# Thirty gathered rows of the first layer given out later: the count EARLY goes from 302 to 272

## The chip, the cores and the metric

The kernel runs on one core of a Trainium2 chip. The metric is the device time of one execution in microseconds (us); lower is better. The core's engines each run their own queue of instructions: TensorE (PE; its weight loads are listed apart as PEld), VectorE (DVE), ScalarE (ACT), GpSimd (POOL) and SyncE (SP), which here issues DMAs. They wait for each other and for DMAs by semaphores.

## The reference

A backbone of two layers over 512 latent tokens and 256 context tokens, width 1024, in float32. Context tokens read only context; latent tokens read both.

```
for i in range(2):
    xl = rmsnorm(hl, norm1_g[i]) * (1 + scale) + shift      # latent; the same for the context (xc)
    yl, yc = even_mixer(...) if i == 0 else odd_mixer(...)  # mLSTM + differential attention; windowed attention with sinks
    hl = hl + gate * yl                                     # output projection inside the mixer
    xl = rmsnorm(hl, norm2_g[i]) * (1 + scale) + shift
    hl = hl + gate * peer(xl)
    if i == 0:
        hc = hc + gate * yc
        hc = hc + gate * peer(rmsnorm(hc) ...)
out = rmsnorm(hl, final_g)
```

The part that matters is `peer`, a layer of 16384 experts of one neuron each. For each token, 8 heads pick 16 experts each by product keys (128 x 128 keys), so 128 pairs of rows (u, v) per token:

```
a = einsum('nd,nhkd->nhk', x, u[eidx])        # 128 dot products of 1024 for each token
w = gate * gelu(a)
y = einsum('nhk,nhkd->nd', w, v[eidx])        # 128 rows, weighted and added
```

## The kernel before

Tokens are handled in blocks of 128: two of context, four of latent tokens. The program runs in this order: the context through the first mixer, its output projection and its choice of experts; the latent tokens through the first mixer (`even`); their output projection (`out_proj`, line 836); `peer` of the first layer (line 1340); the second layer's windowed attention (`odd`, line 1183) and its output projection; `peer` of the second layer.

**Two ways to compute the experts.** For three of the four latent blocks of the first layer (384 tokens) all experts are computed, *densely*: the loop over 128 key blocks j takes 128 experts at a time. TensorE multiplies the 384 tokens by the block's u rows (`dA`, line 217), ScalarE applies Gelu (`dz`), VectorE multiplies with the gates (`dz`, line 1168), which are zero for experts that weren't picked, and splits the result into a high and a low part (`dw`, lines 1171 and 1172); TensorE multiplies by the block's v rows and adds into `dacc` (line 1178). The rows themselves are loaded (`draw`) and split too (`dhi` on ScalarE, `dlo` on VectorE or GpSimd, lines 1122 and 1123). The last four j (TAIL) are accumulated block by block. Behind the loop, for each of the three blocks, `resid` (line 1046) computes `hm`, the sum times a gate row `m` (line 1052), and adds it to the residual `hr` (line 1053).

For the two context blocks and the last latent block the picked rows are *gathered*. The generator `gather` (line 1003) hands out one row per token at each `next(rows)`: an indirect DMA that GpSimd issues (line 1010; 128 x 1024 float32, 524,288 bytes) into a ring of five buffers `uv`, and one pass on VectorE. For each block come 128 u rows (a dot product with the token, `junkv` and `pa`, line 1023), then 128 v rows (weighted and added into `pacc`, line 1036). Three blocks make 768 such steps, in one fixed order: block by block, u before v. In these texts each such step is called a row. The buffers for `hm`, `hr` and `m` of `resid` come from the same ring of five.

**Where the rows are given out.** The 768 are spread over five places by counts. EARLY rows are handed out in `run` (line 1447) ahead of the latent mixer, with a late priority: they fill VectorE and DMA time wherever the mixer and the output projection leave room. GROWS, 48, come beside the building of the gates (`beside`, line 1362). LATE, 64, come inside `odd`. What is left is spread over the dense loop:

```
left, done = 256 * len(gat) - done - GROWS[l] - late, 0
...
while done < min(left * (j + 2) // GEND, left):
    next(rows)
```

with GEND = 124, each batch held until the low part of `dw` of block j has been issued.

**What sets the order.** The program's text gives the instructions in one order with priorities; a scheduler with its own simulated timeline then decides, before the kernel is run, in which order each engine's instructions stand. An engine executes its queue strictly in that order. So a row given out at one place of the text can stand elsewhere in the queues.

**Around the two ends.** In `out_proj` each of the four latent blocks gets its product `ops` (line 223, four column quarters), VectorE multiplies it with a gate row (`ot`, line 852) and adds it to the residual (`oh`, line 853). Then each block is normed (`norm`, lines 372 to 381: the squares on ScalarE, L377; `xn` on VectorE, lines 379 and 381), transposed on TensorE (`xps`, line 388) and split into a high part on ScalarE (`xth`, line 393) and a low part on VectorE (`xtl`, line 394). `xn` has two buffers. Then the first score projection of `peer` begins (`pqps`, line 217).

Behind the dense part, the two context blocks are loaded again and normed (`xn`; here line 381's addition runs on GpSimd) and transposed into `xt` (copied by ScalarE, line 390); their keys are TensorE's `okps` (line 210). The latent blocks' norms start from `hr`. A few small constants for the attention are made on VectorE: `bfc` (line 1213) and the sinks `snp`, `snk`, `snr` (lines 1205 to 1210). `rt` (line 725) belongs to the rotation of the first queries and keys of the heads.

Of the kernel before, what the change touches and what calls it, by code (L numbers as in the profile page):

```python
# [24 lines left out]
SEGS = [(0, 1, 16), (1, 2, 8), (2, 4, 5), (4, 8, 3), (8, 16, 1)]  # L25
NCAND = sum((b - a) * n for a, b, n in SEGS)
UPRE = 18, 27
EARLY = 302
GROWS = 48, 0
LATE = 64  # L30
F5 = [], [5]
# [79 lines left out]
class Kern:  # L111
# [1299 lines left out]
    def run(self, out):  # L1411
# [12 lines left out]
        with self.mixing():  # L1424
            with self.tc.tile_pool(name="even", bufs=1, reuse_waits="tile") as self.pe:
# [20 lines left out]
                with self.later():  # L1446
                    for _ in range(EARLY):
                        next(rows)
# [4 lines left out]

        self.peer(0, xt, 2, gat, rows, EARLY, LATE, put)
        with self.phase("n1c"):
# [93 lines left out]
```

## Time and profile before

| | us |
|---|---|
| median of three runs | 4182.2 (4175.84 to 4185.61) |
| the profiled execution, by the same clock as the runs | 4186.29 |
| span of its trace (first to last instruction) | 4184.5 |
| TensorE busy | 3808.1 (91%) |
| VectorE busy | 3281.6 (78%) |
| GpSimd busy | 2266.9 (54%) |
| ScalarE busy | 1526.5 (36%) |
| 512 gathers of u rows, GpSimd's time for them | 670.2 |
| 512 gathers of v rows, GpSimd's time for them | 684.1 |

The profile is of one execution, the table's second line; the sums below are made against it. Busy times of engines overlap, so they do not add up to the span. The 1024 gathers are those of both layers.

### The profile page before, as it was taken

To read this page: it belongs to the slowest core of one execution; us is meant where nothing else is said; L and a number is where in the kernel's file an instruction comes from. 1 tells how busy PE (TensorE), PEld (TensorE's weight loads), DVE (VectorE), ACT (ScalarE), POOL (GpSimd) and SP (SyncE) were. 2 spreads that over 40 slices of the span, in tenths; PEclk is the share of its full clock that TensorE was granted. 3 is DMA by queue.
4 is the path that set the end of the run, shared out by engine and by line. 5 is a ranking of instruction groups with operands and counts; after the bars stand their busy time and mean duration, and the time that the engine had idled before them with its cause. 6 is when DMAs were issued, how large, how long until landed. Compare 5 with 4: busy or idle time off the path is not lost.

```text
span 4184.5 us, 56313 instructions
## 1 busy us (share of the span) xinstructions
PE 3808.1 (91%) x19774; PEld 3252.5 (78%) x19780; DVE 3281.6 (78%) x5763; ACT 1526.5 (36%) x2798; POOL 2266.9 (54%) x1644
## 2 busy tenths in 40 slices
PE   8988777758899899999999889999999999999999
PEld 5776554546687799999889777777887899999987
DVE  4259888977988899999989987537955977777788
ACT  3322322412156433333333324332366333333333
POOL 1016767554453588778778563004531766666664
PEclk9999988878999999999999999999999999999999
DMA  5556888786339999989899995423346978788778
GB/s 193 171 201 207 314 316 308 263 314 234 129 121 371 361 326 346 350 310 343 317 332 331 341 332 194 154 90 112 117 161 241 347 275 285 275 288 278 280 266 314
DMA packets 389674, 1099.30 MB, mean 263 GB/s; under 512 B 32959, under 2 KB 140807, under 8 KB 383246
## 3 DMA queue, kind: packets, MB, share of 16 engines
q0 software_dynamic: 147456, 536.94, 35.4%
q1 hardware_dynamic: 232142, 497.95, 34.8%
q10 hardware_dynamic: 9792, 60.82, 3.5%
q8 instruction: 155, 2.54, 0.2%
q14 instruction: 129, 1.06, 0.1%
HBM read 1024.18 MB, written 71.40 MB: 262 GB/s over the span
## 4 chain that ended last, share of the span: by engine, by line
PE 55%; DMA 14%; DVE 13%; issue 10%; POOL 7%; ACT 2%; SPq 0%; POOLq 0%; ACTq 0%; DVEq 0%
PE dacc L1178 19%; PE dA L217 17%; DMA uv<-in_pr_u_dram,ix 4%; POOL uv L1010 4%; DMA uv<-in_pr_v_dram,ix 3%; PE pqps L217 2%; DMA draw<-in_uT_dram 2%; PE ops L223 2%; PE gps L1108 2%; DVE junkv L1023 2%; PE oo L1335 1%; PE gds L1091 1%; PE ops L1305 1%; PE modps L252 1%; PE vps L223 1%
## 5 line engine op out<-in xcount | busy, mean ns | idle before, releaser
L1178 PE MATMUL dacc<-dhi,dw 128*128 128x512 f32 x3072 | 986.6, 391 | 5.6 <-ACT dw L1171 3.8
L1010 POOL DMA_INDIRECT uv<-in_pr_u_dram,ix x512 | 670.2, 1309 | 463.0 <-DVE pa L1023 330.4
L1010 POOL DMA_INDIRECT uv<-in_pr_v_dram,ix x512 | 684.1, 1336 | 399.6 <-DVE pacc L1036 274.3
L1023 DVE CUSTOM_DVE_ANT_0 junkv<-uv,x 128x1024 bf16<-128x1024 f32 x512 | 695.1, 1358 | 60.1 <-DMA uv<-in_pr_u_dram,ix 55.9
L1036 DVE SCALAR_TENSOR_TENSOR pacc<-uv,pw,pacc 128x1024 f32<-128x1024 f32 x508 | 701.3, 1381 | 42.0 <-DMA uv<-in_pr_v_dram,ix 38.1
L1178 PEld LDWEIGHTS dacc<-dhi,dw 128*128 128x128 f32 x3072 | 578.5, 188 | 122.5 <-ACT dw L1171 4.5
L1123 POOL TENSOR_TENSOR dlo<-draw,dhi 128x1024 fp32r<-128x1024 f32 x210 | 542.3, 2583 | 211.4 <-ACT dhi L1122 207.7
L1122 ACT CAST dhi<-draw 128x1024 fp32r<-128x1024 f32 x467 | 489.5, 1050 | 445.2 <-issue 176.1
L1178 PE MATMUL dacc<-dlo,dw 128*128 128x512 f32 x1536 | 603.9, 393 | 7.2 <-DVE dlo L1123 7.2
L1168 DVE TENSOR_TENSOR dz<-dz,dG 128x384 f32<-128x384 f32 x256 | 406.5, 1601 | 79.0 <-ACT dz L1138 75.1
L1171 ACT CAST dw<-dz 128x384 fp32r<-128x384 f32 x256 | 131.4, 514 | 708.2 <-PE dacc L1178 690.3
L217 PE MATMUL dA<-xth,dhi 128*128 128x384 f32 x1688 | 335.3, 340 | 11.6 <-ACT dhi L1122 9.8
L1123 DVE TENSOR_TENSOR dlo<-draw,dhi 128x1024 fp32r<-128x1024 f32 x257 | 322.2, 1254 | 27.5 <-ACT dhi L1122 26.7
L1178 PEld LDWEIGHTS dacc<-dlo,dw 128*128 128x128 f32 x1536 | 289.1, 188 | 66.2 <-DVE dlo L1123 9.7
L217 PEld LDWEIGHTS dA<-xth,dhi 128*128 128x128 f32 x1688 | 306.5, 189 | 28.7 <-ACT dhi L1122 10.2
L217 PE MATMUL dA<-xtl,dhi 128*128 128x384 f32 x1688 | 327.4, 335 | 0.0
L217 PE MATMUL dA<-xth,dlo 128*128 128x384 f32 x1688 | 326.6, 334 | 0.8 <-POOL dlo L1123 0.8
L217 PEld LDWEIGHTS dA<-xtl,dhi 128*128 128x128 f32 x1688 | 296.7, 188 | 0.1
L217 PEld LDWEIGHTS dA<-xth,dlo 128*128 128x128 f32 x1688 | 295.6, 188 | 1.2 <-POOL dlo L1123 1.1
L1172 DVE TENSOR_TENSOR dw<-dz,dw 128x384 fp32r<-128x384 f32 x256 | 162.8, 636 | 151.5 <-ACT dw L1171 151.5
L1108 PEld LDWEIGHTS gps<-ghot 128*128 128x128 f32 x1536 | 202.2, 192 | 49.9 <-issue 21.9
L196 POOL TENSOR_TENSOR wlo<-wraw,whi 128x1024 fp32r<-128x1024 f32 x55 | 132.9, 2418 | 194.7 <-ACT whi L195 121.3
(341 smaller groups left out, 6044.9 us busy)
## 6 DMA issues: line engine op xcount, KB each, us to landing
draw<-in_pr_v_dram SPq DMA_DIRECT2D x256, 512.0 KB
draw<-in_uT_dram SPq DMA_DIRECT2D x211, 512.0 KB
wraw<-in_wb_dram SPq DMA_DIRECT2D x150, 512.0 KB
gd<-gch ACTq DMA_DIRECT2D x48, 1024.0 KB
dG<-gd SPq DMA_DIRECT2D x30, 1536.0 KB
wraw<-in_mod_t_dram SPq DMA_DIRECT2D x48, 512.0 KB
wraw<-in_uT_dram SPq DMA_DIRECT2D x45, 512.0 KB
wraw<-in_mod_w_dram SPq DMA_DIRECT2D x32, 512.0 KB
```

The source lines that it names most:

```text
L196: eng.tensor_tensor(lo, raw, hi.bitcast(F32), op=OP.subtract)
L217: self.nc.tensor.matmul(ps, w[wi][:, k, :], x[xi][:, k, 0:T], start=(i == 0), stop=(i == 23))
L1010: nc.gpsimd.indirect_dma_start(out=t, out_offset=None, in_=a[table], in_offset=bass.IndirectOffsetOnAxis(ap=ix[:, c:c + 1], axis=0))
L1023: nc.vector.tensor_tensor_reduce(out=junk, in0=u, in1=x, op0=OP.mult, op1=OP.add, scale=1.0, scalar=0.0, accum_out=A[:, c:c + 1])
L1036: nc.vector.scalar_tensor_tensor(acc, v, W[:, c:c + 1], acc, op0=OP.mult, op1=OP.add)
L1108: nc.tensor.matmul(ps[0][:, t0 % 8 + t, :], h[0][:, t, :], h[1][:, t, :], start=True, stop=True)
L1122: nc.scalar.copy(hi, raw)
L1123: eng.tensor_tensor(lo, raw, hi.bitcast(F32), op=OP.subtract)
L1168: nc.vector.tensor_tensor(z3, z3, self.G[:, :, j % JG, :], op=OP.mult)
L1171: nc.scalar.copy(wh, z)
L1172: i = nc.vector.tensor_tensor(wl, z, wh.bitcast(F32), op=OP.subtract)
L1178: self.nc.tensor.matmul(acc[b][:, h, :], w[wi][:, 128 * b:128 * b + 128], v[vi][:, 512 * h:512 * h + 512], start=(j == 0 and i == 0), stop ...
```

## The change

One number: of the 768 rows of the first layer, 272 and not 302 are handed out ahead of the latent mixer. GROWS and LATE stay, so the rest, which the dense loop spreads, is 384 and not 354.

```diff
 UPRE = 18, 27
-EARLY = 302
+EARLY = 272
 GROWS = 48, 0
 LATE = 64
```

Where the rows come to stand is decided by the scheduler, so here is the order of the instructions of both kernels at three places. (`uv<-in_pr_u_dram` is a gather of u rows, `uv<-in_pr_v_dram` one of v rows; `x21` means that the instruction stands 21 times in a row; a row's dot product shows as two lines, `junkv,pa` and `pa`.)

GpSimd's queue from the last part of the latent mixer to the start of the choice of experts, as one piece of the difference:

```order
 L736 MEMSET qpd 64x512
 L1010 DMA uv<-in_pr_v_dram,ix 128x1024 x59
-L1010 DMA uv<-in_pr_u_dram,ix 128x1024 x51
+L1010 DMA uv<-in_pr_u_dram,ix 128x1024 x21
 L196 TENSOR_TENSOR wlo<-wraw,whi 128x1024 x4
 L955 MEMSET sel 128x4
```

The 59 gathers of v rows in front stay; of 51 gathers of u rows 21 stay.

VectorE's queue at the end of the output projection of the first layer, before (`oh_6039` to `oh_6041` are the residuals of three of the four blocks, `x_3582` the context block whose dot products the rows make):

```order
L852 TENSOR_TENSOR ot<-ops,mr 128x256
L379 SCALAR_TENSOR_TENSOR xn<-oh_6039,rstd,mr 128x1024
L1023 ISA junkv,pa<-uv,x_3582 128x1024
L1023 ISA pa 128x1
L853 TENSOR_TENSOR oh_6041<-oh_6041,ot 128x256
L379 SCALAR_TENSOR_TENSOR xn<-oh_6040,rstd,mr 128x1024
L381 TENSOR_TENSOR xn<-xn,mr 128x1024
L1023 ISA junkv,pa<-uv,x_3582 128x1024
L1023 ISA pa 128x1
L852 TENSOR_TENSOR ot<-ops,mr 128x256
```

The same place of the changed kernel (`oh_5919` to `oh_5922` are the residuals of the blocks):

```order
L852 TENSOR_TENSOR ot<-ops,mr 128x256
L853 TENSOR_TENSOR oh_5920<-oh_5920,ot 128x256
L379 SCALAR_TENSOR_TENSOR xn<-oh_5919,rstd,mr 128x1024
L381 TENSOR_TENSOR xn<-xn,mr 128x1024
L379 SCALAR_TENSOR_TENSOR xn<-oh_5920,rstd,mr 128x1024
L852 TENSOR_TENSOR ot<-ops,mr 128x256
L381 TENSOR_TENSOR xn<-xn,mr 128x1024
L853 TENSOR_TENSOR oh_5921<-oh_5921,ot 128x256
L852 TENSOR_TENSOR ot<-ops,mr 128x256
L853 TENSOR_TENSOR oh_5922<-oh_5922,ot 128x256
L394 TENSOR_TENSOR xtl<-xps,xth 128x8x128 x2
```

Between the projection's products and norms stood dot products of rows; now none do. The first 16 rows of this block stand earlier on VectorE in both kernels, in the same places.

VectorE's queue behind the dense loop, before (the first line here are the last rows behind the last `dw`; `dacc_10198` to `dacc_10200` are the three dense blocks' sums):

```order
L1123 TENSOR_TENSOR dlo<-draw,dhi 128x1024
L1036 SCALAR_TENSOR_TENSOR pacc<-uv,pw,pacc 128x1024 x10
L1213 TENSOR_SCALAR bfc<-cst 128x128 x4
L1052 TENSOR_TENSOR hm<-dacc_10198,m_18841 128x1024
L1036 SCALAR_TENSOR_TENSOR pacc<-uv,pw,pacc 128x1024
L1053 TENSOR_TENSOR hr<-hr,hm 128x1024
L1052 TENSOR_TENSOR hm<-dacc_10199,m_18841 128x1024
L1053 TENSOR_TENSOR hr<-hr,hm 128x1024
L1052 TENSOR_TENSOR hm<-dacc_10200,m_18841 128x1024
L1205 TENSOR_SCALAR snr<-snr 128x16
L379 SCALAR_TENSOR_TENSOR xn<-xn,rstd,mr 128x1024
```

The same place of the changed kernel:

```order
L1123 TENSOR_TENSOR dlo<-draw,dhi 128x1024
L1036 SCALAR_TENSOR_TENSOR pacc<-uv,pw,pacc 128x1024 x10
L1213 TENSOR_SCALAR bfc<-cst 128x128 x4
L1036 SCALAR_TENSOR_TENSOR pacc<-uv,pw,pacc 128x1024 x5
L379 SCALAR_TENSOR_TENSOR xn<-xn,rstd,mr 128x1024
...
L1208 SCALAR_TENSOR_TENSOR snk<-snp,cst,snk 128x16
L1036 SCALAR_TENSOR_TENSOR pacc<-uv,pw,pacc 128x1024 x22
L1052 TENSOR_TENSOR hm<-dacc_10078,m_18841 128x1024
L1052 TENSOR_TENSOR hm<-dacc_10079,m_18841 128x1024
L1053 TENSOR_TENSOR hr<-hr,hm 128x1024 x2
L1052 TENSOR_TENSOR hm<-dacc_10080,m_18841 128x1024
```

The first `hm` stood behind 15 rows and the four `bfc`; now it stands behind 19 rows, the context norm, the sink constants and 22 rows more. Counted over the whole queue, 338 rows stand between the first and the last `dw` before (the 351st to the 688th of the 768), and 343 in the changed kernel (the 321st to the 663rd); behind the last `dw` and ahead of the attention's own rows (LATE) stand 16 before and 41 now. The queues of TensorE, ScalarE and SyncE read almost the same in both, but for SyncE's loads behind the dense loop: `m` and `hr` stood ahead of the context's loads and now stand behind them (`mr`, `xn<-h`, `snr`, three weights, `mrow`). On ScalarE the squares of `hr` stand ahead of the copies of the context's transposes (L390) in both. On TensorE `okps` stands behind the third block's transposes in both.

## Rows read from the trace of the kernel before

**Rows 1.** The page: span, and busy time of each engine.
```profile
span 4184.5 us, 56313 instructions
PE 3808.1 (91%) x19774; PEld 3252.5 (78%) x19780; DVE 3281.6 (78%) x5763; ACT 1526.5 (36%) x2798; POOL 2266.9 (54%) x1644
```
**Rows 2.** Windows: length, PE PEld DVE ACT POOL busy, granted clock, DMA share, GB/s.
```profile
921.00:993.00 72.00, 49.78 (x218) 41.39 (x217) 62.17 (x104) 11.95 (x22) 39.60 (x34) 0.84 0.93 345
1350.00:1400.00 50.00, 39.82 (x248) 34.25 (x248) 32.47 (x52) 26.77 (x37) 15.99 (x14) 0.93 1.03 399
1450.00:2300.00 850.00, 841.78 (x4242) 764.38 (x4242) 784.05 (x754) 306.55 (x410) 674.15 (x396) 1.00 0.92 331
2390.00:2453.00 63.00, 38.69 (x156) 29.07 (x156) 46.23 (x44) 14.88 (x31) 34.20 (x23) 0.78 0.91 337
2453.00:2560.00 107.00, 98.06 (x618) 82.66 (x617) 98.00 (x116) 42.78 (x122) 62.98 (x74) 0.98 0.91 332
```
**Rows 3.** Dense part: chain, then (1450 to 2300 us) gather queue, VectorE's rows.
```profile
1450.34 4.12 PE dacc L1178 x18
1454.46 4.18 PE dA L217 x24
...
q0 software_dynamic: 42531, 154.87, 49.7%
...
L1036 DVE SCALAR_TENSOR_TENSOR pacc<-uv,pw,pacc 128x1024 f32<-128x1024 f32 x146 | 231.3, 1584 | 1.0
```
**Rows 4.** Lines from 926 to 993.5 us: busy, mean ns, idle and releasers.
```profile
L223 PE MATMUL ops<-wraw,xt 128*128 128x256 f32 x162 | 37.9, 394 | 6.3 <-DVE ot L852 4.5 <-DMA wraw<-in_wb_dram 1.8
L388 PE MATMUL xps<-cst,xn 128*128 128x128 f32 x32 | 6.9, 389 | 13.5 <-DVE xn L381 13.5
L217 PE MATMUL pqps<-xth,whi 128*128 128x512 f32 x2 | 1.2, 696 | 2.5 <-DVE xtl L394 2.5
...
L1023 DVE CUSTOM_DVE_ANT_0 junkv<-uv,x 128x1024 bf16<-128x1024 f32 x30 | 36.8, 1228 | 6.8 <-DMA uv<-in_pr_u_dram,ix 6.6
```
**Rows 5.** Behind the dense part: VectorE in time order, lines 2366.5:2393, gathers 2366:2388.
```profile
2366.32 0.56 DVE L1172 TENSOR_TENSOR dw<-dz,dw 128x384 fp32r<-128x384 f32 x1 [0.67 <-ACT dw L1171]
2393.07 0.62 DVE L1213 TENSOR_SCALAR bfc<-cst 128x128 bf16<-128x128 f32 x4
2394.50 1.23 DVE L1052 TENSOR_TENSOR hm<-dacc,m 128x1024 f32<-128x1024 f32 x1 [0.81 <-DMA m<-modd]
2403.18 1.28 DVE L379 SCALAR_TENSOR_TENSOR xn<-xn,rstd,mr 128x1024 f32<-128x1024 f32 x1
2408.88 2.39 DVE L1208 SCALAR_TENSOR_TENSOR snk<-snp,cst,snk 128x16 bf16<-128x16 bf16 x1
...
2452.88 0.55 DVE L725 TENSOR_TENSOR rt<-rps,cst 128x384 f32<-128x384 f32 x1
...
L1036 DVE SCALAR_TENSOR_TENSOR pacc<-uv,pw,pacc 128x1024 f32<-128x1024 f32 x15 | 19.3, 1288 | 3.9 <-DMA uv<-in_pr_v_dram,ix 3.7
L1123 DVE TENSOR_TENSOR dlo<-draw,dhi 128x1024 fp32r<-128x1024 f32 x3 | 3.7, 1219 | 0.0
...
L1010 POOL DMA_INDIRECT uv<-in_pr_v_dram,ix x12 | 16.7, 1392 | 6.1 <-DVE pacc L1036 4.0 <-issue 2.1
```
**Rows 6.** Behind the dense part: ScalarE, GpSimd, TensorE in order of time.
```profile
2400.97 1.06 ACT L377 ACTIVATE junk<-xn 128x1024 bf16<-128x1024 f32 x1 [25.76 <-DMA xn<-h]
2403.95 1.04 ACT L377 ACTIVATE junk<-hr 128x1024 bf16<-128x1024 f32 x1
2408.94 1.01 ACT L390 COPY xt<-xps 128x1024 f32<-128x1024 f32 x1 [1.93 <-PE xps L388]
...
2404.54 2.34 POOL L381 TENSOR_TENSOR xn<-xn,mr 128x1024 f32<-128x1024 f32 x1 [1.08 <-DVE snp L1207]
...
2406.94 1.97 PE L388 MATMUL xps<-cst,xn 128*128 128x128 f32 x8 [16.50 <-POOL xn L381]
2414.37 10.12 PE L210 MATMUL okps<-xt,wraw 128*128 128x256 f32 x32 [1.10 <-ACT xt L390]
```

## The prediction

> **What bounds the kernel now.** I read the page first, then the table of windows stage by stage, then the waits and the order of time at the two ends of the change. TensorE is busy in 91% of the span [rows 1], so what counts is where it is not.
>
> The dense part of the first layer is TensorE's: 841.78 of 850 us busy, at the full clock [rows 2], and its chain is nothing but 4.18 us of `dA` and 4.12 us of `dacc` by turns, 8.30 us for one of 128 key blocks [rows 3]. Beside it VectorE is busy 784.05 us (66 idle) and the DMA engines 0.92 of the time (68 us idle) at 331 GB/s: both have room, but little.
>
> The latent output projection is otherwise: from 926 to 993.5 us TensorE sits idle for 6.3 + 13.5 + 2.5 = 22.3 us, waiting for VectorE (`ot`, `xn`, `xtl`) and once for a weight, while VectorE works through 30 gathered rows, 36.8 us of them [rows 4], and the DMA share is 0.93 [rows 2].
>
> A third place matters, which the words of the change do not name: the seam between the dense part and the second layer. From 2390 to 2453 us TensorE is busy 38.69 of 63 us [rows 2]. What releases it starts with `hm`, the residual of the dense blocks (L1052), at 2394.50 [rows 5].
>
> **The change, part by part.** Nothing is computed less: 30 rows, each one gather on GpSimd, 0.52 MB of DMA and one VectorE pass, are given out later.
>
> *Out of the projection.* GpSimd's order shows 21 gathers for 51 there. VectorE's first 16 rows stand where they stood, so up to about 925 us nothing changes; the 30 after that are gone. Of TensorE's 22.3 us the 6.3 before `ops` should go, as `ot` and `oh` no longer stand behind rows. Of the 16.0 us around the four norms a part stays: the third norm hangs on ScalarE's order and on the write of the first `xn` out of its buffer (two buffers for four blocks), and its own steps get no shorter by an empty queue. I take 6 of the 16 as gained, so **12 us gained**; bounds: 4.5 (only the waits for `ot`) and all 22.3.
>
> *Into the dense part.* Here I counted VectorE's order instead of trusting the loop. Between the first and the last `dw` stand 688 - 350 = 338 rows before and 663 - 320 = 343 after: only **5 of the 30** arrive there. The other 25 stand behind the last `dw`: 16 before, 41 now. For the 5: the gather queue moved 154.87 MB, that is 295 rows of 0.524 MB, in 49.7% of 850 us [rows 3], 1.43 us of DMA a row, 7 us in all, and a pass is 1.58 us of VectorE, 8 us in all, against 68 and 66 us idle. TensorE hides them; without that cover they would be 8 us. I take 1 us; bounds 0 and 8.
>
> *Into the seam.* Before, VectorE starts the last `dw` at 2366.32, runs 15 rows and 3 splits until 2393.07, and `hm` follows at 2394.50, just after TensorE ends the last `dacc` at 2390.4 (its next work, at 2406.94, follows 16.50 us of idling [rows 6]): that run of rows was covered. Its price is (26.2 - 3.7)/15 = 1.5 us a row [rows 5]. Now VectorE has 19 rows, the context norm, the sink constants, 22 rows, and only then `hm`. The 4 extra rows in front cost nothing, since the context norm waits for its loads anyway: ScalarE got `xn` at 2400.97 after 25.76 us of waiting [rows 6], and VectorE ran it at 2403.18. The last constant ends at 2408.88 + 2.39 = 2411.2, where the 22 rows can start. They take 22 x 1.5 = 33 us, so `hm` starts at 2444 instead of 2394.5: 50 us late. Bounds for a row: 1.29 us (VectorE's own time for one in this run) and 1.9 us ((16.7 + 6.1)/12, the cadence of GpSimd's gathers there) [rows 5].
>
> What is queued behind it: on ScalarE the squares of `hr`, and behind them, in both orders, the copies of the context's transposes (`xt`); so the context's keys, which need nothing of `hm`, wait on it too [rows 6]. On TensorE the third transpose, then `okps`, stand in line. On GpSimd 18 gathers are followed by the latent adds. On SyncE the loads of `m` and `hr` now stand behind those for the context, and the next ten weight loads behind them.
>
> What comes back: `okps` began at 2414.37, 19.9 us after `hm` [rows 5, 6], with the context's norms in between, which now lie ahead. What is left is two `hm` and two `hr` (4 x 1.23), ScalarE from the square to `xn` (2403.18 - 2400.97 = 2.2), `xn` (1.28), the GpSimd add (2.34) and the transpose (1.97): 12.7 us, so 7 come back. From there to the end of the heads the same rows stand as before (15 up to `rt` at 2452.88); TensorE is busy 98.06 of 107 us there [rows 2], so at most 9 us can be made up; I take 4. Seam: 50 - 7 - 4 = **39 us lost**. Low end: 28 for the rows, 12 for the 16.7 us from `hm`'s old start to 2411.2 (were the constants done 4 us sooner), less 7 and 9: 24. High end: 42 + 17 - 7 = 52.
>
> *Sum.* -12 + 1 + 39 = +28 us. The profiled execution took 4186.29 us, of which the trace spans 4184.5 [rows 1]; it lies 4.1 us over the median of the three runs, 4182.2. So 4214 for such an execution and **4210 us** for the median, 0.67% slower. A measurement of this kernel can tell about 0.2%, 8.4 us, from no change.
>
> One rule bears on the low end. In one window the DMA engines moved 399 GB/s over 50 us [rows 2], at which a row of 524,288 bytes takes 1.31 us, close to VectorE's 1.29. The Trainium skill (DMA: Bandwidth & Descriptors, section "Where 436 GB/s comes from") says that transfers between HBM and SBUF are bound at some 358 GB/s for a core. By it a row takes no less than 1.46 us, 22 of them 32 us, and the low end of the seam rises by 4 us; the window contradicts it, so my low end stays.
>
> **The rivals.**
> *It does what its words say* (the other side). The 30 rows lie in the dense part, TensorE hides them, the projection gains. For it: 30 x 1.58 = 47 us of VectorE and 30 x 1.43 = 43 us of DMA would fit into 66 and 68 us idle. Against it: VectorE's order, in which 25 of them come after the last `dw`. It decides where `hm` does not wait for them, that is, if the seam costs under 11 us. Then 4182 - 12 + 1 = 4171 us, or 4160 with all of the projection's waits. 7%.
>
> *The seam is cheap and the projection rich.* Rows at 1.29 us and 9 us made up (24 lost) against 22 gained: 4184 us, no change. For it: the splits are over by then, and the 0.91 DMA share in the seam [rows 2] leaves some time. Against it: the constants would have to end 4 us sooner, and the norms' part in the projection's waits would have to vanish. 12%.
>
> *The seam loses, and the dense part with it.* 5 rows more on a VectorE at 92%, and block borders at other places: up to 8 us of TensorE's time, with rows at 1.9 us: 4182 - 4 + 8 + 52 = 4238 us. For it: TensorE already lost 8 us in 850 [rows 2]. Against: 5 rows in 338 are 1.5%. 10%.
>
> **How the numbers follow.** The forecast holds 71%: 4210 us, by itself 4192 to 4226. With the rivals: slower by over 0.2% 81%, within 12%, faster 7%. For 8 in 10 the range runs from the cheap seam to just short of the last case: 4183 to 4232 us.
>
> **What would show it.** In the changed kernel's trace: 21 gathers beside the projection and little idle time before `ops`; the first score projection (`pqps`) and the last `dacc` each some 12 us earlier; 22 rows in one run on VectorE before the first `hm`, which starts some 50 us after the last `dacc` (4 before); TensorE idle for over 50 us at the seam, the context's `okps` after `hm`; from `rt` on everything late by about 28 us. The prediction is wrong if `hm` comes within 15 us of the last `dacc`, if the projection gains more than 22 us, or if the heads make up far more than 9 us.

## The result and the profile after

The changed kernel takes 4216.47 us (median of four runs, 4211.49 to 4221.36), the kernel before, in four runs beside it, 4180.51 us: a ratio of 1.0082, interval 1.0068 to 1.0097. It is 36 us slower; 28 were forecast, and 4216 lies in the range 4183 to 4232. The profiled execution took 4215.46 us. That of before, at 4186.29, lies 5.8 us over its median here, so the difference of the two traces, 29.2 us, is some 7 us short of that of the medians.

The page of the changed kernel, span and busy times:

```profile
span 4213.7 us, 56308 instructions
PE 3800.7 (90%) x19774; PEld 3245.7 (77%) x19780; DVE 3288.7 (78%) x5763; ACT 1524.6 (36%) x2798; POOL 2274.4 (54%) x1644
```

The work is the same, and no engine's busy time differs by more than 8 us. TensorE is even busy 7.4 us less, so it sits idle 36.6 us longer. To find the place I set marks into both traces, the start or end of a group that exists in both (first `ops` of the latent projection, first `pqps`, first `gps` of the gates, first and last `dacc`, first `hm`, first `okps`, first `rt`), and took the differences of neighbours:

| stage, by TensorE's and VectorE's marks | before | after | difference |
|---|---|---|---|
| start to first `ops` | 901.0 | 900.3 | -0.7 |
| projection: first `ops` to first `pqps` | 91.7 | 75.5 | -16.2 |
| choice of experts: to first `gps` | 178.0 | 179.1 | +1.1 |
| gates: to first `dacc` | 225.5 | 229.6 | +4.1 |
| dense part: to the end of the last `dacc` | 994.2 | 992.0 | -2.2 |
| to the first `hm` | 4.1 | 60.9 | +56.8 |
| to the first `okps` | 19.9 | 12.7 | -7.2 |
| to the first `rt` | 38.5 | 36.0 | -2.5 |
| rest | 1731.6 | 1727.6 | -4.0 |

**Projection.** First the one stretch of before that [rows 2] lacks, the whole projection, then the changed kernel's windows: the projection, the dense part, from the last `dacc` to behind the first `hm`, and the heads. The columns are those of [rows 2].

```profile
901.00:992.70 91.70, 64.93 (x265) 53.41 (x265) 70.39 (x120) 11.65 (x22) 43.35 (x38) 0.82 0.95 358
```
```profile
900.30:975.80 75.50, 59.47 (x264) 51.06 (x265) 35.92 (x58) 10.87 (x21) 8.95 (x9) 0.90 0.60 231
...
1436.00:2286.00 850.00, 843.54 (x4251) 765.90 (x4250) 787.78 (x770) 305.15 (x410) 687.03 (x399) 1.00 0.93 331
2376.50:2439.00 62.50, 2.17 (x9) 1.81 (x10) 46.66 (x46) 3.29 (x8) 32.03 (x27) 0.52 0.88 330
2486.00:2593.00 107.00, 95.76 (x601) 80.04 (x600) 96.60 (x116) 41.06 (x120) 61.97 (x74) 0.98 0.91 333
```

Of the 16.2 us in the projection 10.7 are idle time of TensorE (91.70 - 64.93 = 26.8 before, 75.50 - 59.47 = 16.0 after). The other 5.5 are the same matmuls in less time, 59.47 for 64.93 us, at a granted clock of 0.90 for 0.82 (means between the two levels, 1.2 and 2.4 GHz: the window behind the last `dacc`, where TensorE does nearly nothing, has 0.52, the dense part 1.00). Such a mean counts idle time too. What counts is how long TensorE worked at the lower level: 18.92 us before (in 901.0:904.8, 908.3:915.1, 928.7:932.1 and 973.1:992.7) and 10.20 us in the changed kernel (in 900.3:904.7, 921.7:925.2 and 966.1:972.9). In the changed kernel 8 `ops` matmuls take 3.78 us at the lower level (from 900.30) and 48 take 10.63 us at the higher (from 906.12), 0.47 and 0.22 us each; so by an estimate the difference is worth about half of it, 4.4 of the 5.5 us. The stretch that [rows 4] showed, in the changed kernel, then `ops` in the whole projection, before and in the changed kernel:

```profile
L223 PE MATMUL ops<-wraw,xt 128*128 128x256 f32 x166 | 36.2, 380 | 0.0
L388 PE MATMUL xps<-cst,xn 128*128 128x128 f32 x32 | 5.3, 336 | 7.2 <-DVE xn L381 7.2
```
```profile
L223 PE MATMUL ops<-wraw,xt 128*128 128x256 f32 x232 | 58.0, 414 | 24.3 <-DMA xt<-yd 13.5 <-DVE ot L852 9.0 <-DMA wraw<-in_wb_dram 1.8
```
```profile
L223 PE MATMUL ops<-wraw,xt 128*128 128x256 f32 x232 | 54.3, 398 | 20.1 <-DMA xt<-yd 13.7 <-DMA wraw<-in_wb_dram 4.3 <-DVE ot L852 2.0
L217 PE MATMUL pqps<-xth,whi 128*128 128x512 f32 x3 | 1.1, 494 | 2.5 <-DVE xtl L394 2.5
```

In the stretch of [rows 4] the 6.3 us before `ops` are gone. In the whole projection less is gained there. Leaving out the wait for `xt`, which ends with the first `ops`, where the stage begins, TensorE waits before `ops` for 9.0 + 1.8 = 10.8 us before and 4.3 + 2.0 = 6.3 us now: less for VectorE, but more for a weight. That is 4.5 us. Of the 13.5 us before the transposes 6.3 are gone; the 2.5 us before `pqps` stay.

**Seam.** VectorE of the changed kernel in order of time, then its 22 rows as a group; then ScalarE, one line of GpSimd, and TensorE there. They answer to [rows 5, 6].

```profile
2379.60 0.63 DVE L1213 TENSOR_SCALAR bfc<-cst 128x128 bf16<-128x128 f32 x4
2381.16 1.28 DVE L1036 SCALAR_TENSOR_TENSOR pacc<-uv,pw,pacc 128x1024 f32<-128x1024 f32 x1 [0.93 <-DMA uv<-in_pr_v_dram,ix]
...
2390.93 1.28 DVE L1036 SCALAR_TENSOR_TENSOR pacc<-uv,pw,pacc 128x1024 f32<-128x1024 f32 x1 [1.32 <-DMA uv<-in_pr_v_dram,ix]
2392.14 1.28 DVE L379 SCALAR_TENSOR_TENSOR xn<-xn,rstd,mr 128x1024 f32<-128x1024 f32 x1
...
2400.70 0.23 DVE L1208 SCALAR_TENSOR_TENSOR snk<-snp,cst,snk 128x16 bf16<-128x16 bf16 x1
...
2437.43 2.35 DVE L1052 TENSOR_TENSOR hm<-dacc,m 128x1024 f32<-128x1024 f32 x2
...
L1036 DVE SCALAR_TENSOR_TENSOR pacc<-uv,pw,pacc 128x1024 f32<-128x1024 f32 x22 | 28.3, 1285 | 8.4 <-DMA uv<-in_pr_v_dram,ix 7.6 <-DVE pacc L1036 0.2
```
```profile
2384.86 1.06 ACT L377 ACTIVATE junk<-xn 128x1024 bf16<-128x1024 f32 x1 [23.63 <-DMA xn<-h]
2440.95 1.06 ACT L377 ACTIVATE junk<-hr 128x1024 bf16<-128x1024 f32 x1 [51.97 <-DVE hr L1053]
2443.93 1.91 ACT L390 COPY xt<-xps 128x1024 f32<-128x1024 f32 x2
...
2398.00 2.34 POOL L381 TENSOR_TENSOR xn<-xn,mr 128x1024 f32<-128x1024 f32 x1 [1.40 <-DVE snp L1207]
...
2396.65 1.97 PE L388 MATMUL xps<-cst,xn 128*128 128x128 f32 x8 [20.19 <-POOL xn L381]
2438.80 1.94 PE L388 MATMUL xps<-cst,xn 128*128 128x128 f32 x8 [40.17 <-DVE hm L1052]
2448.32 1.97 PE L388 MATMUL xps<-cst,xn 128*128 128x128 f32 x8 [7.58 <-POOL xn L381]
2450.08 9.17 PE L210 MATMUL okps<-xt,wraw 128*128 128x256 f32 x32
```

TensorE is busy 2.17 of the 62.50 us behind the last `dacc` (the window above). It transposes the first context block at 2396.65, then waits 40.17 us for `hm`, which VectorE starts at 2437.43, when the 22 rows are done. ScalarE meanwhile waits 51.97 us for `hr`, with the copies of the finished transposes behind it in its queue. So it's not only the context's copies that hang on `hm`, as I had written: by the trace the second context block's transposes do so themselves. Their input was ready at 2400.34 (GpSimd's addition above), and they read nothing of `hm`. By the program it is the place of their output: `xps` lies in PSUM, the memory for TensorE's products, in a pool that is opened when that of the three `dacc` is closed, and `hm` is what reads `dacc`. No run tests this reading apart.

One sentence on the orders, ahead of the prediction, is wrong: `okps` stands behind the third block's transposes in the changed kernel only. Before, it came at 2414.37 [rows 6], behind two blocks' transposes, at 2406.94 [rows 6] and here:

```profile
2411.30 1.97 PE L388 MATMUL xps<-cst,xn 128*128 128x128 f32 x8 [2.39 <-POOL xn L381]
```

In the changed kernel the third block's transposes, at 2448.32, stand ahead of it and wait 7.58 us more for a latent block's norm.

### The profile page after: what moved, and what is told of

The parts are those of the page before. It is cut to its first block, busy times and chain, and to the rows that moved or that the text cites. A ratio compares the mean times of both kernels' runs of the same rounds, so it can differ in the third digit from the quotient of the medians.

```text
span 4213.7 us, 56308 instructions
## 1 busy us (share of the span) xinstructions
PE 3800.7 (90%) x19774; PEld 3245.7 (77%) x19780; DVE 3288.7 (78%) x5763; ACT 1524.6 (36%) x2798; POOL 2274.4 (54%) x1644
## 4 chain that ended last, share of the span: by engine, by line
PE 57%; DVE 14%; DMA 12%; issue 9%; POOL 6%; ACT 2%; SPq 0%; POOLq 0%; ACTq 0%; DVEq 0%
PE dacc L1178 20%; PE dA L217 18%; POOL uv L1010 4%; DMA uv<-in_pr_v_dram,ix 4%; PE ops L223 3%; DMA uv<-in_pr_u_dram,ix 3%; PE pqps L217 2%; PE gps L1108 2%; DMA draw<-in_uT_dram 2%; DVE junkv L1023 2%; PE gds L1091 1%; PE oo L1335 1%; DVE pacc L1036 1%; PE modps L252 1%; PE ops L1305 1%
## 5 line engine op out<-in xcount | busy, mean ns | idle before, releaser
L1010 POOL DMA_INDIRECT uv<-in_pr_u_dram,ix x512 | 681.7, 1331 | 434.0 <-DVE pa L1023 306.1
L1023 DVE CUSTOM_DVE_ANT_0 junkv<-uv,x 128x1024 bf16<-128x1024 f32 x512 | 706.2, 1379 | 46.8 <-DMA uv<-in_pr_u_dram,ix 42.3
L1172 DVE TENSOR_TENSOR dw<-dz,dw 128x384 fp32r<-128x384 f32 x256 | 153.7, 600 | 143.5 <-ACT dw L1171 143.5
```

The costliest lines, as they stand in the source:

```text
L1010: nc.gpsimd.indirect_dma_start(out=t, out_offset=None, in_=a[table], in_offset=bass.IndirectOffsetOnAxis(ap=ix[:, c:c + 1], axis=0))
L1023: nc.vector.tensor_tensor_reduce(out=junk, in0=u, in1=x, op0=OP.mult, op1=OP.add, scale=1.0, scalar=0.0, accum_out=A[:, c:c + 1])
L1172: i = nc.vector.tensor_tensor(wl, z, wh.bitcast(F32), op=OP.subtract)
```

## The experiments

The experiments came in three groups. Beside each the kernel before ran again on the same chip; its medians were 4178.75, 4177.93 and 4178.22 us. Stage times are of one profiled execution of each kernel, which lay between 5 us below (e302l39) and 10 us above (e296hm) that kernel's median.

### drop30: the gain without the price

```diff
             for c in range(128):
+                if l == 0 and hb == 1 and 90 <= c < 120:
+                    continue
                 v = fetch("pr_v", ix, c)
...
-            left, done = 256 * len(gat) - done - GROWS[l] - late, 0
+            left, done = 256 * len(gat) - done - GROWS[l] - late - 30 * (l == 0), 0
```

(against the changed kernel)

> The changed kernel with 30 of the second context block's v rows left out (so their share of the result is missing); VectorE's order at the projection is that of the changed kernel, behind the last dw that of the kernel before (15 rows ahead of hm). It gives the gain at the projection without its price. My theory (price at the seam, 22 rows ahead of hm): pqps 12 to 17 us earlier than before, hm within 6 us of the last dacc, 4164 to 4169 us. Rival (the gain at the projection is given back by the gate building and the dense part, whatever the seam does): pqps early, but the last dacc not, 4176 to 4182 us.

Measured: 4168.88 us for 4178.75, ratio 0.9981 (0.9969 to 0.9992). The projection takes 76.4 us, the gates 231.2. My theory's range held, at its edge: without the rows at the seam the change would be a gain, of some 8 to 10 us. The rival has a part in it, since the gates took 5.7 us more than in the trace of before. One wait makes that up, the first `dA` of the dense part's own u rows for their load and split. Waits of TensorE in the gate stage, in the kernel before, the changed one, drop30, and two kernels told below:

```profile
PE dA L217 <- ACT dhi L1122: 7.3, 1, 7.3
```
```profile
PE dA L217 <- ACT dhi L1122: 11.3, 1, 11.3
```
```profile
PE dA L217 <- ACT dhi L1124: 12.2, 1, 12.2
```
```profile
PE dA L217 <- ACT dhi L1122: 4.8, 1, 4.8
```
```profile
PE dA L217 <- ACT dhi L1122: 2.5, 1, 2.5
```

The fourth is hmfirst25, which gives out the same rows in that stage as the changed kernel and drop30, and waits 4.8; the fifth is e302l39, which there is the kernel before, and waits 2.5 for that one's 7.3. So this wait differs by some 5 to 7 us between kernels that give out the same rows there. narrow30 and nogather30, told next, have EARLY 302 as well and wait 7.7 and 10.1 us, so the two groups overlap: it isn't tied to the change. ScalarE's split waits in its turn for the load of the rows; what makes that late, I did not find out.

### narrow30 and nogather30: whose time was it at the projection

Both are edits of the kernel before (EARLY 302) on the 30 rows that the change moves; ahead of the "..." narrow30, behind it nogather30:

```diff
                 u = fetch("pr_u", ix, c)
                 junk = pg.tile([128, D], BF16, name="junkv", tag="junkv", bufs=1)
+                n = 64 if l == 0 and hb == 1 and 16 <= c < 46 else D
-                nc.vector.tensor_tensor_reduce(out=junk, in0=u, in1=x, op0=OP.mult, op1=OP.add,
+                nc.vector.tensor_tensor_reduce(out=junk[:, :n], in0=u[:, :n], in1=x[:, :n], op0=OP.mult,
...
-                u = fetch("pr_u", ix, c)
+                u = x if l == 0 and hb == 1 and 16 <= c < 46 else fetch("pr_u", ix, c)
```

> The kernel before with the 30 dot products that the change moves narrowed from 1024 to 64 columns (the rest of those products is left out); their 30 gathers stay, and the order of VectorE at the projection is nearly that of before. If TensorE waits there for VectorE's time: pqps 10 to 16 us earlier, 4165 to 4171 us. If it is the DMA traffic of the gathers (late weights, late stores): pqps at most 4 us earlier, 4176 to 4181 us.

> The kernel before without the 30 gathers that the change moves; their VectorE passes stay and read the token block in place of the row (so these products are wrong ones). If TensorE waits at the projection for VectorE's time: pqps at most 4 us earlier, 4176 to 4181 us. If it is the gathers' DMA traffic, or VectorE waiting for gathered rows (6.8 us of its idle time there): pqps 7 to 16 us earlier, 4165 to 4174 us.

Measured: 4172.25 us (ratio 0.9983, 0.9972 to 0.9993) and 4172.17 us (0.9982, 0.9972 to 0.9992). narrow30 lies between its two cases, 1 us above the range of the first; nogather30 lies in the range of its second. So neither VectorE's passes nor the gathers are the whole. The projection's window in narrow30, then in nogather30:

```profile
899.40:981.50 82.10, 61.55 (x264) 50.78 (x265) 43.06 (x120) 10.88 (x21) 39.55 (x39) 0.85 1.00 394
```
```profile
898.10:982.40 84.30, 63.24 (x264) 52.85 (x265) 69.74 (x120) 11.17 (x22) 8.44 (x8) 0.88 0.55 208
```

From 91.7 us, the projection gets 9.6 us shorter with VectorE's 30 passes narrowed and 7.4 without the 30 gathers; together 17, and the change, which takes out both, has 16.2. (e302l39, told below, leaves the projection as it was and takes 93.4 us, so these differences are good to some 2 us.) The gathers' part reaches TensorE through VectorE as well: in the projection VectorE waits 12.1 us for gathered rows before and 4.9 in nogather30, while TensorE's wait for weights stays, 1.8 and 1.6 us. In narrow30 the DMA share is 1.00 at 394 GB/s and VectorE waits 22.7 us for rows: with its passes short, it is the gathers that it waits for.

### hmfirst25: the same rows, `hm` ahead of them

```diff
             left, done = 256 * len(gat) - done - GROWS[l] - late, 0
+            after = 25 if l == 0 else 0
+            left -= after
...
                 for b in range(nd):
                     put(bb + b, self.resid(m5, acc[b].rearrange("p h d -> p (h d)"), bb + b))
+                for _ in range(after):
+                    next(rows)
```

(against the changed kernel)

> The changed kernel with all its work, but the last 25 rows of the dense part's share are written behind resid, so hm stands ahead of them on VectorE (16 rows between the last dw and hm, as before). My theory (it is the order: hm behind 22 rows): hm within 8 us of the last dacc, the rows are taken up by the heads at a price of at most 9 us, 4165 to 4178 us, faster than before. Rival (the volume: 25 rows more behind the dense part cost their VectorE and DMA time of 1.5 us each wherever they stand): 4203 to 4216 us, as the changed kernel.

Measured: 4194.66 us, ratio 1.0045 (1.0029 to 1.0060): between the two, some 20 us faster than the changed kernel and 16 slower than the kernel before. `hm` comes 7.6 us after the last `dacc`, as I expected, and `rt` 65 us after it (62 before, 110 in the changed kernel). But the heads, from the first `rt` to the last score product of the attention (`ops` of line 1305), take 316.8 us for 291.0. I expected at most 9 us there. TensorE's transposes of the last latent block, in hmfirst25, then in the kernel before, there with GpSimd's addition ahead of it:

```profile
2594.06 1.97 PE L388 MATMUL xps<-cst,xn 128*128 128x128 f32 x8 [21.82 <-POOL xn L381]
```
```profile
2567.47 2.45 POOL L381 TENSOR_TENSOR xn<-xn,mr 128x1024 f32<-128x1024 f32 x1 [14.86 <-PE opt L1329]
...
2586.04 1.04 PE L388 MATMUL xps<-cst,xn 128*128 128x128 f32 x8
```

There is a second thing that I hadn't seen in the trace of before. The last latent block is itself a gathered one: its norm can start only when the last of the 768 rows has been added. Before, that norm was ready at 2567.47 + 2.45 = 2569.9 and TensorE came for it at 2586.04: 16 us to spare. In hmfirst25 the last row comes 49 us later, counted from the last `dacc` (218.1 us to the block's `hm` for 169.0; 25 rows at 1.96 us), the spare time is used up, and TensorE waits 21.82 us. The rival was half right: the volume counts, above that slack.

### e302l39: `hm` late, no more rows

```diff
-EARLY = 272
+EARLY = 302
-LATE = 64
+LATE = 39
```

(against the changed kernel)

> The kernel before (EARLY 302) with LATE 39 for 64: all work is done, the projection is untouched and no more rows stand behind the dense part than before (75 for 80), but hm stands behind 20 rows and the sink constants and 16 rows more. The order alone (hm late): hm 24.5 + 17 x 1.66 = 53 us after the last dacc, 49 later than before, less some 10 that come back as in the changed kernel: 39 us slower, about 4218 us. The volume alone (what counts is when the last of the 768 rows is done, which is no later than before): the same as before, 4172 to 4187 us.

Measured: 4212.66 us for 4177.93, ratio 1.0082 (1.0069 to 1.0095): the same loss as the change itself, with the projection untouched (93.4 us) and the last row earlier than before (the last block's `hm` 158.3 us after the last `dacc` for 169.0). TensorE's second context transposes, and VectorE's `hm`:

```profile
2432.77 2.35 DVE L1052 TENSOR_TENSOR hm<-dacc,m 128x1024 f32<-128x1024 f32 x2
...
2434.13 1.94 PE L388 MATMUL xps<-cst,xn 128*128 128x128 f32 x8 [32.12 <-DVE hm L1052]
```

`hm` comes 54.1 us after the last `dacc` (53 expected), and from there to `rt` it is 46.2 us for 58.4 before. The order alone is enough to lose 35 us.

### e287 and e290: smaller doses

EARLY 287 and EARLY 290, nothing else changed.

> EARLY 287, half the change; all work is done. By VectorE's order hm stands behind 18 rows, the constants and 7 rows more; 10 more rows than before stand behind the last dw. The projection gains about half, 8 us. The order: hm 24.5 + 8 x 1.66 = 38 us after the last dacc, 34 later, less 10: +24 - 8 = 16 us slower, about 4195 us. The volume: 10 rows of 1.85 us are 18 us, inside the 20 us that the last block's norm had to spare: only the gain is left, about 4171 us.

> EARLY 290 alone, the partner of e290hm: the same 12 rows taken from the projection, but hm stands behind 18 rows, the constants and 5 rows more (23 behind the last dw, where e290hm has 16 and then hm). All work is done. If hm's place is what parts them: hm some 33 us after the last dacc (6 in e290hm), and 15 to 22 us slower than e290hm, 4180 to 4187 us, no faster than before. If the gain of e290hm came from the smaller number of rows at the projection alone: 4163 to 4169 us.

Measured: e287 4186.86 us for 4177.93, ratio 1.0017 (1.0008 to 1.0026); e290 4179.96 for 4178.22, 1.0004 (0.9993 to 1.0015), so no change. `hm` comes 37.3 and 27.7 us after the last `dacc` (38 and 33 expected); the projection takes 84.0 and 83.0 us, some 8 less than before. The loss of e287, 9 us, is about half of what I put on it, but has the sign of the order's theory, not of the volume's. The break-even lies near EARLY 290.

### e290hm, e296hm, e284hm, e278hm: `hm` first, and how many rows behind it

The edit of hmfirst25 with EARLY 290, 296, 284, 278 and 8, 4, 14, 20 rows behind `resid`, so that `hm` has 16 rows ahead of it each time, as in the kernel before.

> EARLY 290 with the last 8 rows of the dense part's share written behind resid; all work is done. hm stands behind 16 rows as in the kernel before, and 89 rows stand behind the last dw for 80. If hm's place and the slack of the last block's norm (some 20 us, 10 rows) are all there is at the seam, only the gain of 12 rows at the projection is left, 4 to 8 us: about 4173 us, a little faster than before. If the rows behind hm cost TensorE something from the first one on (1 us a row, as 25 rows cost 25 us of the attention): 4173 + 9 = 4182 us.

> EARLY 296 with 4 rows behind resid: 16 rows ahead of hm, 85 behind the last dw; 6 rows off the projection. All work is done. No wait for the last block's norm; only the gain of 6 rows, 3 to 4 us: 4168 to 4176 us. If it is as fast as e290hm (4165), the gain there isn't the projection's alone.

> EARLY 284 with 14 rows behind resid: 16 rows ahead of hm as before, 95 behind the last dw (80 before, 89 in e290hm, 105 in hmfirst25). All work is done. If the last block's norm has some 20 us to spare and a row costs 1.9 us of it: 15 rows are 28 us, 8 over; the projection gains 3 us more than in e290hm: some 5 us slower than e290hm, 4166 to 4174 us. If a row behind hm cost nothing: 4162 us.

> EARLY 278 with 20 rows behind resid: 100 rows behind the last dw. All work is done. By the slack of 20 us and 1.9 us a row: 38 - 20 = 18 us over, the projection gains 6 us more than in e290hm: 12 us slower than e290hm, about 4177 us (4172 to 4186), with TensorE waiting some 15 us for the last block's norm. If a row behind hm cost nothing: 4159 us.

| kernel | rows behind the last `dw` | us | ratio (interval) | projection | last `dacc` to last block's `hm` | wait for that block's norm | heads |
|---|---|---|---|---|---|---|---|
| before | 80 | 4178 | | 91.7 | 169.0 | none | 291.0 |
| e296hm | 85 | 4180.63 | 1.0003 (0.9993 to 1.0013) | 94.1 | 182.6 | none | 294.3 |
| e290hm | 89 | 4164.79 | 0.9972 (0.9960 to 0.9983) | 84.5 | 184.8 | none | 293.1 |
| e284hm | 95 | 4175.67 | 0.9990 (0.9978 to 1.0002) | 82.9 | 201.3 | 6.95 | 301.4 |
| e278hm | 100 | 4182.93 | 1.0010 (0.9999 to 1.0022) | 81.2 | 210.4 | 18.71 | 314.3 |
| hmfirst25 | 105 | 4194.66 | 1.0045 (1.0029 to 1.0060) | 74.4 | 218.1 | 21.82 | 316.8 |

The waits' rows of e284hm and e278hm:

```profile
2575.98 1.97 PE L388 MATMUL xps<-cst,xn 128*128 128x128 f32 x8 [6.95 <-POOL xn L381]
```
```profile
2586.07 1.97 PE L388 MATMUL xps<-cst,xn 128*128 128x128 f32 x8 [18.71 <-POOL xn L381]
```

The slack is there: no wait up to 89 rows (e290hm), where the last block's `hm` comes 15.8 us later than before, then one that grows. It is smaller than I took it, 16 and not 20 us, and e284hm is 11 us slower than e290hm, not 5; e278hm lies where I expected it. The other three miss: e290hm is faster than expected, e296hm and e284hm are slower.

Between e290 and e290hm, the same EARLY without and with the edit, the edit shows at its place: from the last `dacc` to the first `rt` it is 76.6 us without and 65.3 with it, and the ratios are 1.0004 and 0.9972. But e290hm is 13 us, or 0.28%, faster than the kernel before, and most of that is not explained by what was edited. By the stages it gains 7.2 us in the projection and loses 2.9 from the last `dacc` to `rt` and 2.1 in the heads; some 2 us are left. The rest lies in stages that the edit leaves nearly alone: its dense part takes 982.7 us, where the others in the table take 987.8 to 997.3, and its first `ops` comes 5.5 us earlier. Its neighbours on both sides, e296hm and e284hm, gain nothing that is clear of noise, and e296hm's projection is no shorter than before (94.1 us, where 3 to 4 us less were expected).

### g78hm: the rows beside the gates

```diff
-GROWS = 48, 0
+GROWS = 78, 0
```

and 8 rows behind `resid`, at EARLY 272.

> EARLY 272 with GROWS 78: the 30 rows go beside the building of the gates, and the last 8 of the dense part's share are written behind resid; all work is done. The projection gains its 15 us. The gate building has VectorE idle for 42 of 229 us and the DMA at 0.72; 30 rows want 47 us of VectorE and 43 us of DMA. If it hides most of them: 4165 to 4172 us, faster than before. If it has no room: 15 to 30 us more in that stage, 4180 to 4195 us.

Measured: 4181.68 us for 4177.93, ratio 1.0011 (1.0002 to 1.0020). That is the case without room. The projection has its gain (74.9 us), and the gates take 248.4 us for 225.5: 30 rows cost 23 us there, 17 to 25 against the other kernels' 223.6 to 231.2. TensorE's waits in that stage:

```profile
PE gds L1091 <- DVE ghot L1095: 17.2, 24, 2.4
PE dA L217 <- POOL dlo L1123: 13.3, 1, 13.3
```

Before, the first of these was 9.3 us, and the second, for a split on GpSimd, wasn't there. That stage has no room. VectorE's idle time there (by the changed kernel's trace 46.7 of 229.6 us, at a DMA share of 0.74, not 42 and 0.72) was no free time: 26.7 us of it are waits for TensorE's `gds`, 12.9 for a split on ScalarE.

## Why the prediction was right, and where it was off

**The place and the sign.** Right, and for the reason given. The 25 rows that VectorE's order puts behind the last `dw` delay `hm`; e302l39 shows that this order alone costs 35 us; in hmfirst25, where `hm` comes first, some 20 us of the loss are gone, and in e290hm against e290 11 us of the stretch behind the last `dacc`. The rival by which the dense part hides all 30 rows fell: `hm` waits for them. The cheap seam fell with 47 us there, the dense part's loss with a dense part no longer than before. One link was missing: the second context block's transposes wait for `hm` themselves.

**Seam: 39 forecast, 47.1 measured** (56.8 - 7.2 - 2.5). The working was `hm` 50 us late, 7 back before `okps`, 4 in the heads. What came back was nearly right (7.2 for 7, and 2.5 up to `rt` for 4, of which the heads give back 0.5); the lateness of `hm` was mis-sized by 7 us in two terms. The rows start 24.3 us after the last `dacc` (2400.85 - 2376.5), not 20.8 (2411.2 - 2390.4): I had put the rows ahead of the context norm at nothing, but they came at 2.4 us each (2381.16 to 2390.93, five of them), waiting for their gathers, and held up the norm. And the 22 rows took 36.6 us, 1.66 each and not 1.5: VectorE worked 28.3 us and waited 7.6 for gathers. The Trainium skill (DMA: Bandwidth & Descriptors, section "Where 436 GB/s comes from") has transfers between HBM and SBUF bound at some 358 GB/s for a core, from which I had estimated no less than 1.46 us for a row. That did not bind here: rows took 1.66 at 299 GB/s, and narrow30's 82 us at 394 GB/s go over its figure.

**Projection: -12 forecast, -16.2 measured.** The idle time was nearly as I had it, 10.7 us less for 12, but not quite where: 4.5 us less before `ops` (6 taken, as a weight came later) and 6.3 of the 16 around the norms (6 taken). What I left out is the clock: the same matmuls took 5.5 us less, 10.20 us of their work and not 18.92 being at the lower level. That TensorE waited for VectorE holds, but VectorE's passes are only half of it: without the gathers alone VectorE waits less for rows, and the projection is 7.4 us shorter.

**Dense part: +1 forecast, -2.2 measured.** In 850 us TensorE is busy 843.54 us with the five more rows, 841.78 before [rows 2]: hidden, as assumed. The difference of the stage is within what it varies by (narrow30, with the rows of before there, takes 989.0 us for 994.2).

**Not in the sum.** The gates' +4.1 is the wait shown under drop30, which varies as much between kernels that are alike there. In the heads I saw VectorE's load, but not that the last latent block's norm waits for the last row. It cost nothing here. Counted from the last `dacc`, the last block's `hm` comes 46.9 us later than before (2592.42 - 2376.5 = 215.9 for 169.0), 31 beyond its 16 us to spare; TensorE comes 47 late itself, for the order. The larger of the two counts, not the sum. Once `hm` is put first, the second is the bound. That the sum, 28 us, came so near to the 29.2 between the traces is luck in part: a price 8 us too small stood against a gain 4 us too small and a dense part put 3 us too high. The 36 us between the medians are more, since the profiled execution of before lay 5.8 us above its median.

## What to carry to other kernels

A count that says where work is given out doesn't say where it stands: read the order of the engine that does the work, and look for what is queued behind it. Filler (work that is given out to fill idle time) that is moved to a later stage with little room can land behind it, as 25 of 30 rows did here. What then costs is the short instruction behind the filler on which the next stage hangs; write that one ahead of the filler. And two delays that lead to the same place counted here by the larger: taking one away showed the next, so look for the last consumer of the filler too.

## What the runs showed that I had not expected

Less idle time went with a higher granted clock: in the projection, with TensorE idle 29% of the time, the same matmuls took 64.93 us, 18.92 of them at the lower level, and with 21% idle 59.47 us, 10.20 of them at the lower level. That is a third of that stage's gain. The mean clock of a window doesn't tell this by itself: nogather30's projection has a higher mean than narrow30's (0.88 for 0.85) and more busy time (63.24 for 61.55 us), at the same 25% of idle time. The transfers reached 394 GB/s over 82 us (narrow30), with the DMA share at 1.00. And a stage with the same instructions differed by several us in a single wait for a load: 7.3 us before and 2.5 in e302l39, which are alike there; 12.2 in drop30 and 4.8 in hmfirst25, which give out the same rows.
